# Which engine writes the low parts of U's first 64 tiles: GpSimd without a break during the search's maxima, VectorE during its sums and key choice

## The chip, the core and the metric

One core of a Trainium2 chip runs the whole program: two transformer-like blocks on 256 tokens of width 1024, in fp32. The time is device microseconds of one launch; before the change the median of three runs is 1352.74 us (1351.55 to 1354.43). TensorE multiplies, VectorE and ScalarE do elementwise work, GpSimd can do elementwise work too, and SyncE's queue (SP) starts most transfers from memory.

## The reference, cut to what matters

The stretch in question is the mixture of 16,384 experts at the end of the first block. Each of 8 heads picks 16 experts from two sets of 128 keys; each token then uses 128 rows of `expert_u` and `expert_v`.

```
q = (xn @ w_query).reshape(bsz, seq, PEER_HEADS, 2, PEER_HALF)
scores = einsum("bshpd,hpnd->bshpn", q, sub_keys)
s_top, i_top = lax.top_k(scores, PEER_TOPK)              # 16 of 128, twice a head
cand = s_top[..., 0, :, None] + s_top[..., 1, None, :]
cand_idx = i_top[..., 0, :, None] * PEER_KEYS + i_top[..., 1, None, :]
best, pos = lax.top_k(cand, PEER_TOPK)
idx = take_along_axis(cand_idx, pos); gates = softmax(best)
act = gelu(einsum("td,ted->te", xt, expert_u[it]))
y = einsum("te,ted->td", gt * act, expert_v[it])
```

The kernel does not gather: it multiplies the tokens with all of U (128 tiles of 128 experts), and sets the gates to zero where an expert was not picked.

## The kernel before, in words

**Split weights.** A product in fp32 is made of three faster ones. Each weight tile (128 x 1024, 512 KB) is loaded by SP's queue into a buffer `raw`. ScalarE writes its high part `hi` (`split_next`, L140), and VectorE or GpSimd the low part `lo = raw - hi` (L142). TensorE then does, for each of 8 blocks of the tile, hi with the tokens' high part, hi with their low part, and lo with their high part (L153 to L155): 24 matmuls a tile. `raw`, `hi` and `lo` have three buffers each, so the high part of tile n+3 waits until TensorE is done with tile n, and a load waits until both parts of the tile three before have been read out.

**Who does the low part.** `plan()` lists all tiles in the order of their use and notes for each whether GpSimd ("G") or VectorE ("V") does its low part. In all other weights it is VectorE. In the first 64 tiles of U the pattern is "GGGV".

**What runs beside it.** While TensorE works on U's first 64 tiles, VectorE finds the experts (`topk`, started by `side`). It works in two rounds of 128 tokens. A round is: the maxima (16 times MAX, MAX_INDEX, MATCH_REPLACE, MAX, MAX_INDEX on 128 scores, L1089 to L1094); the candidate sums (`cand`, L1103, and `sif`, L1109); the maxima of the candidates (L1112 to L1117); and the key choice: `ex` (L1123), whose exponential ScalarE takes (L1124), `ab`, `abf`, `fb` (L1128 to L1142), sums and scaling (`sm`, `exk`, L1145 to L1149), and for each of the two key sets a comparison `oh` with all 16 places (L1155), its product with the indices (L1157), and four halvings (L1160, L1161). The results are transposed on TensorE and copied to `iT`, `jT`, `gh`, `gl` (L1170 to L1173). Next `modulation` begins: 96 loads of `wm` (L1321) from GpSimd's queue, each followed by a weighted sum on VectorE (L1324), which frees the one buffer for the next load. `gates` makes R, E, Ch and Cl (L1199 to L1205), two sets ahead of their use.

**What orders it.** The generators advance one step at a tick, two ticks a tile. A scheduler then places each instruction in its engine's queue; the queues run in order. `behind` puts each step of `topk` behind the last low part that VectorE has been given:

```
i = (self.G if self.order[m][1] else self.V).tensor_sub(lo, raw, hi.bitcast(F32))
if not self.order[m][1]:
    self.last_split = i
...
with self.tc.issue_after(self.last_split.ins):
    r = next(gen)
```

Tiles of U are numbered from 0 here. Gelu (L1179) takes the product of two tiles (a pair) from one of two buffers, and TensorE needs that buffer again two pairs later.

Of the kernel before, what the change touches and what calls it, by code (L numbers as in the profile page):

```python
# [40 lines left out]
class Net:  # L41
# [26 lines left out]
    def plan(self):  # L68

        I = self.I  # L70
        w = I["w_in"]
        o = []

        self.first_ring, self.second_ring = [], []
        bufs = {id(self.first_ring): 3, id(self.second_ring): 1}

        def add(tiles, who, deep=False):
            for n, t in enumerate(tiles):
                ring = self.second_ring if deep and n % 4 == 0 else self.first_ring
                o.append((t, who[n % len(who)] == "G", ring, ring[-bufs[id(ring)]] if len(ring) >= bufs[id(ring)] else -1))  # L80
                ring.append(len(o) - 1)
        add([I["w_xk"][b] for b in range(8)], "V")
        add([I["w_ba"]] + [w[b] for b in range(16, 20)], "V")
        add([I["w_xv"][b] for b in range(4)], "V")
        add([w[b] for b in (*range(12, 16), *range(20, 24))], "V")
        add([I["w_xv"][b] for b in range(4, 8)], "V")
        add([w[b] for b in range(24, 28)], "V")
        add([w[b] for i in range(4) for b in (4 + i, 8 + i)], "V")
        add([w[b] for b in range(0, 4)], "V")
        add([I["w_out"][b] for b in range(8)], "V")  # L90
        add([I["w_xq"][b] for b in range(8)], "V", True)
        add([I["w_xo"][b] for b in range(8)], "V", True)
        add([I["w_pq"][b] for b in range(8)], "V", True)
        add([I["U"][b] for b in range(64)], "GGGV")
        add([I["U"][b] for b in range(64, 128)], "V")
        add([I["V"][b] for b in range(64)], "V")
        add([I["V"][b] for b in range(64, 128)], "V")
        for g in range(4):
            add([I["cv_ab"][4 * g + b] for b in range(4)], "V")
        add([I["cv_g"][b] for b in range(8)], "V")  # L100
        add([I["cv_out"][b] for b in range(8)], "V", True)
        add([I["pl_in"][b] for b in range(16)], "V", True)
        add([I["pl_grp"][b] for b in range(2)], "V")
        add([I["pl_out"][b] for b in range(8)], "V", True)
        self.order = o
        self.pos = self.n_dma = self.n_split = 0
        self.raws, self.tiles = {}, {}
# [1705 lines left out]
```

## Time and profile before

| | |
|---|---|
| median of 3 runs | 1352.74 us |
| profiled execution | 1357.57 us, span 1355.0 us |
| TensorE busy | 1295.6 us (96%), 11212 matmuls |
| VectorE busy | 1013.2 us (75%) |
| ScalarE busy | 643.0 us (47%) |
| GpSimd busy | 182.4 us (13%), of it 120.4 in 48 low parts (2513 ns mean) |
| VectorE's low parts | 343, 424.6 us (1241 ns mean) |
| mean granted clock of TensorE | 0.983 of full speed |

The chain of work that ended last lies on TensorE for 84% of the span and on VectorE for 9%. Busy shares are means over the whole program; the change lies between 315 and 525 us, where the first 64 tiles of U are multiplied.

### The profile page before, as it was taken

How to read it: one execution, taken by the hardware profiler on the slowest of the kernel's cores; microseconds unless marked ns; L12 is line 12 of the kernel's file. 1: busy time of each engine (PE TensorE's matmuls, PEld its weight loads, DVE VectorE, ACT ScalarE, POOL GpSimd, SP SyncE). 2: the span in 40 equal slices, each digit the busy share in tenths (PEclk: the TensorE clock that was granted, in tenths of full speed). 3: DMA queues.
4: the chain of work that ended last, by engine and by line, in shares of the span. 5: the costliest groups of instructions: out<-in, count | busy, mean ns of one | idle time of the engine just before them, and what ended most of it. 6: DMA issues, size and time to landing. Idle time of an engine off the chain costs nothing.

```text
span 1355.0 us, 27261 instructions
## 1 busy us (share of the span) xinstructions
PE 1295.6 (96%) x11212; PEld 1264.5 (93%) x11212; DVE 1013.2 (75%) x1881; ACT 643.0 (47%) x841; POOL 182.4 (13%) x179
## 2 busy tenths in 40 slices
PE   7999979999979989999999999998999999998987
PEld 7999969989979989999999999998999996998987
DVE  7897756456897856888887999985666666667885
ACT  6675335555444534443444434434444444455652
POOL 0000000002655663000000000010000000000000
PEclk9999998999999999999999999998999997999999
DMA  7644324444546656666767676666777772433553
GB/s 237 199 149 127 94 79 155 126 140 140 172 132 190 178 163 224 207 210 206 214 202 222 211 213 198 209 215 207 235 235 233 235 225 70 129 130 111 171 163 118
DMA packets 67340, 239.69 MB, mean 177 GB/s; under 512 B 8146, under 2 KB 8402, under 8 KB 67088
## 3 DMA queue, kind: packets, MB, share of 16 engines
q1 hardware_dynamic: 59536, 212.79, 51.7%
q0 software_dynamic: 7680, 25.17, 5.6%
q8 instruction: 87, 1.43, 0.4%
q14 instruction: 37, 0.30, 0.1%
HBM read 236.88 MB, written 1.05 MB: 176 GB/s over the span
## 4 chain that ended last, share of the span: by engine, by line
PE 84%; DVE 9%; ACT 2%; DMA 2%; issue 2%; SPq 0%; DVEq 0%; ACTq 0%
PE mm L155 12%; PE mm L153 12%; PE mm L154 12%; PE y L1261 9%; PE y L1263 9%; PE y L1262 9%; DVE lo L142 3%; PE mm L185 2%; PE mm L186 2%; PE mm L184 2%; PE mmv L210 1%; PE mmv L212 1%; PE mmv L211 1%; PE G L1213 1%; ACT hi L140 1%
## 5 line engine op out<-in xcount | busy, mean ns | idle before, releaser
L140 ACT ACTIVATE hi<-raw 128x1024 fp32r<-128x1024 f32 x391 | 412.5, 1060 | 565.8 <-PE mm L154 221.9
L142 DVE TENSOR_TENSOR lo<-raw,hi 128x1024 fp32r<-128x1024 f32 x343 | 424.6, 1241 | 182.4 <-ACT hi L140 181.5
L155 PE MATMUL mm<-xbh,lo 128*128 128x256 f32 x1128 | 319.0, 283 | 12.3 <-DVE lo L142 12.2
L153 PE MATMUL mm<-xbh,hi 128*128 128x256 f32 x1128 | 321.1, 285 | 0.9 <-ACT act L1179 0.6
L154 PE MATMUL mm<-xbl,hi 128*128 128x256 f32 x1128 | 317.7, 282 | 0.0
L1261 PE MATMUL y<-xbh,hi 128*128 128x256 f32 x1008 | 285.3, 284 | 3.8 <-ACT hi L140 3.8
L1262 PE MATMUL y<-xbl,hi 128*128 128x256 f32 x1008 | 284.5, 283 | 0.0
L1263 PE MATMUL y<-xbh,lo 128*128 128x256 f32 x1008 | 283.8, 282 | 0.8 <-DVE lo L142 0.8
L155 PEld LDWEIGHTS mm<-xbh,lo 128*128 128x128 f32 x1128 | 213.9, 190 | 13.7 <-DVE lo L142 13.5
L153 PEld LDWEIGHTS mm<-xbh,hi 128*128 128x128 f32 x1128 | 214.4, 190 | 1.4 <-ACT act L1179 0.8
L154 PEld LDWEIGHTS mm<-xbl,hi 128*128 128x128 f32 x1128 | 214.4, 190 | 0.0
L1261 PEld LDWEIGHTS y<-xbh,hi 128*128 128x128 f32 x1008 | 191.1, 190 | 4.0 <-ACT hi L140 4.0
L1263 PEld LDWEIGHTS y<-xbh,lo 128*128 128x128 f32 x1008 | 190.6, 189 | 1.7 <-DVE lo L142 1.0
L1262 PEld LDWEIGHTS y<-xbl,hi 128*128 128x128 f32 x1008 | 191.3, 190 | 0.0
L142 POOL TENSOR_TENSOR lo<-raw,hi 128x1024 fp32r<-128x1024 f32 x48 | 120.4, 2513 | 198.4 <-ACT hi L140 198.1
L153 PE MATMUL mm<-xah,hi 128*128 128x256 f32 x448 | 128.5, 288 | 3.4 <-ACT xah L1384 3.4
L154 PE MATMUL mm<-xal,hi 128*128 128x256 f32 x448 | 127.9, 286 | 0.7 <-DVE xal L1385 0.7
L155 PE MATMUL mm<-xah,lo 128*128 128x256 f32 x448 | 127.9, 286 | 0.5 <-DVE lo L142 0.5
L1321 POOL DMA_DIRECT2D wm<-in_w_mod x96 | 51.7, 539 | 531.1 <-DVE wm L1324 515.3
L153 PEld LDWEIGHTS mm<-xah,hi 128*128 128x128 f32 x448 | 85.0, 190 | 4.7 <-ACT xah L1384 3.6
L155 PEld LDWEIGHTS mm<-xah,lo 128*128 128x128 f32 x448 | 85.1, 190 | 1.8 <-issue 1.0
L154 PEld LDWEIGHTS mm<-xal,hi 128*128 128x128 f32 x448 | 84.9, 190 | 1.8 <-DVE xal L1385 0.9
(463 smaller groups left out, 2183.8 us busy)
## 6 DMA issues: line engine op xcount, KB each, us to landing
raw<-in_U SPq DMA_DIRECT2D x128, 512.0 KB, 3.8
raw<-in_V SPq DMA_DIRECT2D x128, 512.0 KB, 4.2
wm<-in_w_mod POOLq DMA_DIRECT2D x96, 256.0 KB, 4.0
raw<-in_w_in SPq DMA_DIRECT2D x28, 512.0 KB, 3.7
raw<-in_cv_ab SPq DMA_DIRECT2D x16, 512.0 KB, 3.6
raw<-in_pl_in SPq DMA_DIRECT2D x16, 512.0 KB, 4.3
raw<-in_w_xk SPq DMA_DIRECT2D x8, 512.0 KB, 4.9
raw<-in_w_xv SPq DMA_DIRECT2D x8, 512.0 KB, 4.2
```

What stands on the lines that cost most here:

```text
L140: self.A.activation(hi, raw, AF.Copy)
L142: i = (self.G if self.order[m][1] else self.V).tensor_sub(lo, raw, hi.bitcast(F32))
L153: self.P.matmul(ps, lhsT=hi[:, w], rhs=xh[:, k, :], start=(k == 0 and first), stop=False, skip_group_check=True)
L154: self.P.matmul(ps, lhsT=hi[:, w], rhs=xl[:, k, :], start=False, stop=False, skip_group_check=True)
L155: self.last_mm = self.P.matmul(ps, lhsT=lo[:, w], rhs=xh[:, k, :], start=False, stop=(k == KB - 1), skip_group_check=True)
L184: self.P.matmul(o, lhsT=hi[:, c], rhs=xh[:, k, :], start=a, stop=False, skip_group_check=True)
L185: self.P.matmul(o, lhsT=hi[:, c], rhs=xl[:, k, :], start=False, stop=False, skip_group_check=True)
L186: self.P.matmul(o, lhsT=lo[:, c], rhs=xh[:, k, :], start=False, stop=z, skip_group_check=True)
L1261: P.matmul(o, lhsT=hi[:, w], rhs=wh[:, s, :], start=(j == 0 and db % 2 == 0), stop=False, skip_group_check=True)
L1262: P.matmul(o, lhsT=hi[:, w], rhs=wl[:, s, :], start=False, stop=False, skip_group_check=True)
L1263: P.matmul(o, lhsT=lo[:, w], rhs=wh[:, s, :], start=False, stop=(j == 127), skip_group_check=True)
L1321: nc.gpsimd.dma_start(w, self.I["w_mod"][n, :, 512 * c:512 * (c + 1)])
```

## The change

The pattern "GGGV" of U's first 64 tiles is replaced by a list of tiles that are VectorE's; all others are GpSimd's.

```diff
-        add([I["U"][b] for b in range(64)], "GGGV")
+
+        mine = (12, 13, *range(18, 26), 39, 40, *range(45, 53))
+        add([I["U"][b] for b in range(64)], ["V" if b in mine else "G" for b in range(64)])
```

VectorE has 20 of the 64 tiles instead of 16: 12 and 13 in the first round's sums, 18 to 25 in its key choice, 39, 40 and 45 to 52 in the second round. GpSimd has 0 to 11, 14 to 17, 26 to 38, 41 to 44 and 53 to 63 without a break. Since `behind` follows VectorE's last low part, the queues change too. In after, line numbers below the diff are two higher (L142 becomes L144).

VectorE's queue in the first round's key choice, of before, from the comparison of the first key set on (the low part at the end is tile 23's; tile 19's stands two rows ahead of the first):

```order
L1155 TENSOR_TENSOR oh<-abf,iota_3604 128x2048
L1146 RECIPROCAL sm<-sm 128x8
L1157 TENSOR_TENSOR oh<-oh,sif 128x2048
L1147 TENSOR_SCALAR sm<-sm 128x8
L1160 TENSOR_TENSOR oh<-oh 128x1024
L1149 TENSOR_TENSOR exk<-ex,sm 128x8x16
L1160 TENSOR_TENSOR oh<-oh 128x512
L1160 TENSOR_TENSOR oh<-oh 128x256
L1161 TENSOR_TENSOR sel<-oh 128x128
L1155 TENSOR_TENSOR oh<-abf,iota_3604 128x2048
L142 TENSOR_TENSOR lo<-raw,hi 128x1024
```

The same place in after, from the third low part of the choice on (the low parts are those of tiles 20 to 23):

```order
L144 TENSOR_TENSOR lo<-raw,hi 128x1024
L1159 TENSOR_TENSOR oh<-oh,sif 128x2048
L1149 TENSOR_SCALAR sm<-sm 128x8
L144 TENSOR_TENSOR lo<-raw,hi 128x1024
L1162 TENSOR_TENSOR oh<-oh 128x1024
L1151 TENSOR_TENSOR exk<-ex,sm 128x8x16
L1162 TENSOR_TENSOR oh<-oh 128x512
L1162 TENSOR_TENSOR oh<-oh 128x256
L144 TENSOR_TENSOR lo<-raw,hi 128x1024
L1163 TENSOR_TENSOR sel<-oh 128x128
L1157 TENSOR_TENSOR oh<-abf,iota_3604 128x2048
L144 TENSOR_TENSOR lo<-raw,hi 128x1024
```

Ahead of tile 23's low part stood ten instructions of the choice in a row; now at most four stand between two low parts.

GpSimd's queue around the second round's end, of before (`lo` are low parts, `wm` the modulation's loads):

```order
L923 TENSOR_TENSOR oT<-oT,zs 128x512 x2
L142 TENSOR_TENSOR lo<-raw,hi 128x1024 x45
L1321 DMA wm<-in_w_mod 128x512
L142 TENSOR_TENSOR lo<-raw,hi 128x1024
L1321 DMA wm<-in_w_mod 128x512
L142 TENSOR_TENSOR lo<-raw,hi 128x1024 x2
L1321 DMA wm<-in_w_mod 128x512 x61
```

And of after:

```order
L925 TENSOR_TENSOR oT<-oT,zs 128x512 x2
L144 TENSOR_TENSOR lo<-raw,hi 128x1024 x39
L1323 DMA wm<-in_w_mod 128x512
L144 TENSOR_TENSOR lo<-raw,hi 128x1024 x2
L1323 DMA wm<-in_w_mod 128x512
L144 TENSOR_TENSOR lo<-raw,hi 128x1024 x2
L1323 DMA wm<-in_w_mod 128x512
L144 TENSOR_TENSOR lo<-raw,hi 128x1024
L1323 DMA wm<-in_w_mod 128x512 x60
```

The first load still stands behind tile 58's low part; behind it there are now two low parts (59 and 60) before the second load, two before the third (61 and 62) and one behind it (63).

VectorE's queue at the same place, of before, from the last copy of the search on:

```order
L1173 TENSOR_TENSOR gl<-ptk,gh 128x128
L1316 TENSOR_SCALAR silu_c<-silu_c 128x512
L1317 SCALAR_TENSOR_TENSOR silu_c<-tanh_c,silu_c 128x512
L142 TENSOR_TENSOR lo<-raw,hi 128x1024
L1324 SCALAR_TENSOR_TENSOR wm,part<-wm,silu_c 128x512 x2
L142 TENSOR_TENSOR lo<-raw,hi 128x1024 x2
L1324 SCALAR_TENSOR_TENSOR wm,part<-wm,silu_c 128x512
L142 TENSOR_TENSOR lo<-raw,hi 128x1024 x2
L1324 SCALAR_TENSOR_TENSOR wm,part<-wm,silu_c 128x512
```

And of after, up to the low parts of tiles 65 and 66:

```order
L1175 TENSOR_TENSOR gl<-ptk,gh 128x128
L1318 TENSOR_SCALAR silu_c<-silu_c 128x512
L1319 SCALAR_TENSOR_TENSOR silu_c<-tanh_c,silu_c 128x512
L1326 SCALAR_TENSOR_TENSOR wm,part<-wm,silu_c 128x512 x2
L1205 TENSOR_TENSOR Ch<-E,gh 128x512
L1201 TENSOR_TENSOR R<-iota,iT 128x1024
L1207 TENSOR_TENSOR Cl<-E,gl 128x512
L1203 TENSOR_TENSOR E<-iota,jT 128x512
L144 TENSOR_TENSOR lo<-raw,hi 128x1024
L1326 SCALAR_TENSOR_TENSOR wm,part<-wm,silu_c 128x512
L144 TENSOR_TENSOR lo<-raw,hi 128x1024 x2
L1326 SCALAR_TENSOR_TENSOR wm,part<-wm,silu_c 128x512
```

The low parts of tiles 59 and 63 are gone from VectorE, the first two weighted sums follow each other, and four instructions of the gates stand ahead of tile 64's low part.

## Rows read from the trace of the kernel before

**Rows 1.** TensorE's waits, 315 to 525 us: waited for, total us, times, longest.
```profile
PE mm L155 <- DVE lo L142: 11.2, 3, 4.9
```

**Rows 2.** Timeline of TensorE, 373 to 494: start, us, instruction, [idle before, releaser].
```profile
373.39 0.28 PE L154 MATMUL mm<-xbl,hi 128*128 128x256 f32 x1
375.22 0.39 PE L155 MATMUL mm<-xbh,lo 128*128 128x256 f32 x1 [1.54 <-DVE lo L142]
...
383.52 0.28 PE L155 MATMUL mm<-xbh,lo 128*128 128x256 f32 x1
384.42 0.39 PE L153 MATMUL mm<-xbh,hi 128*128 128x256 f32 x1 [0.62 <-ACT act L1179]
...
399.24 0.28 PE L154 MATMUL mm<-xbl,hi 128*128 128x256 f32 x1
404.34 0.58 PE L155 MATMUL mm<-xbh,lo 128*128 128x256 f32 x1 [4.82 <-DVE lo L142]
...
408.31 0.28 PE L155 MATMUL mm<-xbh,lo 128*128 128x256 f32 x1
...
411.95 0.28 PE L153 MATMUL mm<-xbh,hi 128*128 128x256 f32 x1
...
485.26 0.28 PE L154 MATMUL mm<-xbl,hi 128*128 128x256 f32 x1
490.39 0.58 PE L155 MATMUL mm<-xbh,lo 128*128 128x256 f32 x1 [4.86 <-DVE lo L142]
...
493.69 0.28 PE L155 MATMUL mm<-xbh,lo 128*128 128x256 f32 x1
```

**Rows 3.** Windows: us, each engine's busy time, granted clock, DMA share, GB/s.
```profile
381.00:407.00 26.00, 20.48 (x158) 19.86 (x157) 25.62 (x25) 11.89 (x14) 15.59 (x6) 0.89 0.41 116
402.00:403.00 1.00, 0.00 (x0) 0.00 (x0) 1.00 (x1) 0.00 (x0) 1.00 (x1) 0.50 0.00 0
409.00:410.00 1.00, 1.00 (x11) 1.00 (x10) 0.00 (x0) 1.00 (x2) 0.00 (x0) 1.00 0.92 377
```

**Rows 4.** Timeline of ScalarE, 342 to 394.
```profile
342.03 1.06 ACT L140 ACTIVATE hi<-raw 128x1024 fp32r<-128x1024 f32 x1 [1.73 <-PE mm L154]
...
381.10 0.40 ACT L1124 ACTIVATE ex<-ex,rcol 128x128 f32<-128x128 f32 x1 [5.33 <-DVE ex L1123]
...
393.63 1.06 ACT L140 ACTIVATE hi<-raw 128x1024 fp32r<-128x1024 f32 x1 [0.67 <-PE mm L155]
```

**Rows 5.** Timeline of VectorE, 372 to 471.
```profile
372.08 3.09 DVE L142 TENSOR_TENSOR lo<-raw,hi 128x1024 fp32r<-128x1024 f32 x1
...
382.75 2.81 DVE L1142 TENSOR_TENSOR abf<-bi,fb 128x128 f16<-128x128 uint32 x1
...
397.54 3.46 DVE L1155 TENSOR_TENSOR oh<-abf,iota 128x2048 f16<-128x2048 f16 x1
400.93 3.36 DVE L142 TENSOR_TENSOR lo<-raw,hi 128x1024 fp32r<-128x1024 f32 x1
...
412.82 1.23 DVE L142 TENSOR_TENSOR lo<-raw,hi 128x1024 fp32r<-128x1024 f32 x1 [5.56 <-ACT hi L140]
...
470.75 0.74 DVE L1142 TENSOR_TENSOR abf<-bi,fb 128x128 f16<-128x128 uint32 x1
```

**Rows 6.** Timeline of GpSimd, 343 to 421.
```profile
343.17 2.39 POOL L142 TENSOR_TENSOR lo<-raw,hi 128x1024 fp32r<-128x1024 f32 x1 [0.38 <-ACT hi L140]
...
400.46 2.74 POOL L142 TENSOR_TENSOR lo<-raw,hi 128x1024 fp32r<-128x1024 f32 x1 [0.54 <-ACT hi L140]
...
415.96 5.34 POOL L142 TENSOR_TENSOR lo<-raw,hi 128x1024 fp32r<-128x1024 f32 x2 [3.56 <-ACT hi L140]
```

**Rows 7.** Timeline of GpSimd, 517 to 523.
```profile
517.68 0.55 POOL L1321 DMA_DIRECT2D wm<-in_w_mod  x1 [2.03 <-DVE wm L1324]
518.26 4.77 POOL L142 TENSOR_TENSOR lo<-raw,hi 128x1024 fp32r<-128x1024 f32 x2
```

**Rows 8.** Loads of U issued, 330 to 372: KB each, median us to landing.
```profile
raw<-in_U SPq DMA_DIRECT2D x13, 512.0 KB, 3.6
```

## The prediction

> **What bounds the kernel now.** I read the page first: TensorE is busy 96% of the span and its waits are the only idle time that counts. Then I asked for TensorE's waits in the stretch that the diff touches, the first 64 tiles of U (315 to 525 us). There the low parts were late on VectorE three times, 11.2 us in all [rows 1]. The timeline of TensorE [rows 2] turns this into lost time. Undisturbed, 31 matmuls start between 408.31 and 411.95, one each 0.117 us, so a tile of 24 takes 2.82 us. Four places fall off that pace:
> - 373.39 to 375.22: 1.83 us for one pitch, 1.7 lost.
> - 383.52 to 384.42: 0.90 us, 0.8 lost, behind a Gelu on ScalarE (L1179).
> - 399.24 to 404.34: 5.10 us, 5.0 lost. Then 18 matmuls start in 3.97 us (404.34 to 408.31) where 2.12 would do: 1.85 lost. The granted clock is 0.50 there and 1.00 afterwards [rows 3]: TensorE had stood idle, fell from 2.4 to 1.2 GHz, and worked some 4 us before it was back.
> - 485.26 to 490.39: 5.13 us, 5.0 lost, and 15 matmuls in 3.30 us (490.39 to 493.69) instead of 1.76: 1.5 lost.
> Sum: 1.7 + 0.8 + 5.0 + 1.85 + 5.0 + 1.5 = 15.9 us, 1.2% of the span.
>
> The reader is to see next why a low part is late. The high part of tile 23 starts on ScalarE at 393.63 and TensorE wants the low part some 5.7 us later, at 399.24 [rows 2, 4]; VectorE starts it at 400.93 [rows 5]. It stands in VectorE's queue behind the key choice, and those instructions are long: L1142 takes 2.81 us at 382.75 and 0.74 at 470.75; a low part takes 1.23 at 412.82 but 3.36 at 400.93, when GpSimd is inside a low part of its own (400.46, 2.74 long) [rows 5, 6]. From 382.75 to 400.93 there are six such instructions of 2.3 us or more, the first and the last of which are shown. The two engines hold each other up, and VectorE loses about 2.1 us each time. GpSimd suffers less: 2.39 us at 343.17 beside maxima, 2.74 at 400.46 [rows 6].
>
> **The change part by part.**
> *Tiles 18 to 25 and 45 to 52 on VectorE during the sums and the key choice.* GpSimd is then idle, so the lengthening goes. VectorE is busy 25.62 of the 26 us from 381 to 407 [rows 3]. Taking off six times 2.1 (12.6) leaves 13.0, of which two low parts are 2.5, so the choice itself is about 10.5 us. Eight low parts of 1.23 make 9.8: 20.3 us of work in eight tiles (22.6 us). It fits with 2 us over. In the order of after the 10.5 us stand in pieces between the low parts, 1.3 us on the mean; the longest piece, the seven instructions from L1123 to L1142, I estimate at under 3, since L1142 alone is 0.74. A VectorE low part is ready 1.06 + 0.1 + 1.23 = 2.4 us after its high part starts and is wanted 5.7 us after: 3.3 us of cover. So both 5 us waits go, and with them both stretches at 1.2 GHz: 13.4 us. If the cover fails, one tile's wait of 5 us comes back.
> *Tiles 12, 13 and 39, 40 on VectorE during the candidate sums.* The first wait (tile 15) came of it: VectorE was behind with sums lengthened by GpSimd, started tile 15 at 372.08 although its high part was long there, and then took 3.09 us itself [rows 5]. Now tile 15 is GpSimd's and the sums have VectorE alone: 1.7 us go. ScalarE stood 5.33 us at the exponential of the chosen scores (381.10, L1124), waiting for a late VectorE, with Gelu and two high parts queued behind [rows 4]; that made the 0.8 us wait. In after the exponential's operand follows tile 18's low part directly, and ScalarE's table load covers that. So 0.8 go.
> *36 tiles plus eight as GpSimd's alone during the maxima.* The cost of a lone run is 2.4 us a tile on GpSimd against 2.82 on TensorE, so it keeps pace. Latency: the high part starts at 342.03, the low part ends at 345.56 [rows 4, 6], 3.5 us later, wanted after 5.7: 2.2 us of cover. The maxima themselves do not lengthen it: 2.39 us is measured beside a full VectorE queue. Taken as nothing. Bounds: 0, and if each stood at the 2.74 of a contended one, still under 2.82: also 0.
> *Nine two-operand instructions of the gates* (R, E, Ch, Cl, L1199 to L1205) stand among the second round's maxima in both orders. In before the two of L1199 met a pair of low parts (415.96), which took 5.34 instead of 4.8 us [rows 6], 0.27 for each instruction. Nine times 0.27 is 2.4 us of lag against 2.2 of cover, and if one low part bears both, 0.54 each, 4.9: between 0 and 2.7 us. I take 0.2, near the row itself, since gaps of 0.4 us between low parts let GpSimd catch up.
> The Trainium skill, "SBUF — State Buffer", section "SBUF: two separate sides", says that VectorE instructions with two SBUF inputs, or in a two-port mode, and GpSimd's share one port pair, which the first to start holds for its whole instruction. The six long instructions agree with that. By that rule the nine instructions would hold GpSimd for their full lengths, and the sum would be worse by up to about 2 us than with the 0.27 of the row; no run here shows which it is in an unbroken GpSimd run.
> *Tiles 53 to 63 on GpSimd, with three of the modulation's loads in its queue.* This is the one place that gets tighter. The load of wm waits for VectorE's sum over the previous one, and the low parts behind it on GpSimd's queue wait too. In before the second load waited 2.03 us (517.68), and the next two low parts ran back to back, 4.77 us [rows 7]; TensorE just did not wait. Now tiles 59 and 63 also go through GpSimd (in before VectorE did them), 2.4 us each, with the second load between 60 and 61 and the third between 62 and 63. Following the queue with before's durations, tile 61's low part ends 0.3 us and tile 63's 0.85 us too late, and tile 64's, behind four gate instructions on VectorE, about level. Bounds: 0, and 4 us (two waits of 2.03 passed on in full). I take 1.0.
> *What else is queued.* A raw buffer is free only after the low part has read it, and GpSimd's low part ends 1.2 us later than VectorE's. The round trip of three buffers is landing 3.6 us [rows 8] + high part 1.06 + low part 2.4 + about 0.4 of hand-overs = 7.5 us for three tiles, which TensorE takes 8.46 for. Hidden, 1.0 us of cover. SP's order of loads is the same. Behind tile 64 only neighbours change places in VectorE's order, where TensorE has no low-part waits now: nothing.
> Sum: 13.4 + 1.7 + 0.8 - 0.2 - 1.0 = 14.7 us gained.
> The profiled execution took 1357.57 us with a span of 1355.0, 4.8 us above the runs' median of 1352.74; the waits lie in the program, so I take the 14.7 us off both: 1342.9 for its like, and 1352.74 - 14.7 = **1338.0 us** for the median.
>
> **The rivals.**
> *GpSimd runs late in places.* For it: 2.03 us wait before the load, tight already, and the nine gate instructions. Against: 2.2 us of cover elsewhere. If the two loads' waits come in full (4), the nine cost 2, and one stretch falls to 1.2 GHz again (1.85 + about 2), 5 to 10 us of the 15.9 are eaten: 1342 to 1347.
> *VectorE's instructions in the choice are not shortened.* If their length had another cause than GpSimd, the choice needs 23.1 us, with eight low parts 32.9 in 22.6 us: 10.3 late less 3.3 of cover, 7.0 a round, with the slow clock 8.7; twice that is 17.4 for 15.9 taken away: 1354, no change. Against: the same line, L1142, at 2.81 and 0.74 in the same program.
> *The buffers' round trip becomes the bound (slower).* Place: all-GpSimd runs, 44 tiles, some 14 round trips. If landing rises over 4.6 us, each 1 us more costs 14 us; above 4.6 + 15.9/14 = 5.7 us the kernel is slower than before. At 6.2 it gives 1338 + 22 = 1360. For it: nothing breaks up the runs any more. Against: landing 3.6 us beside the same loads now.
>
> **How the numbers follow.** Forecast (1334 to 1342): 0.68. Late GpSimd (1342 to 1348): 0.19. No shortening: 0.06. Round trip or something like it: 0.05. Better than 1334: 0.02. The likeliest gives 1338. Its bounds are 1336.8 (nothing lost in the loads or the gates) and some 1342 (4.0 in the loads and a little of the 2.7 in the gates); the other cases reach on, so the range is 1333 to 1347, which leaves out the last two rivals. A measurement of this kernel can tell about 0.2% (2.7 us) from no change. Faster: 0.68 + 0.19 + 0.02 = 0.89; within 0.2%: 0.06; slower: 0.05.
>
> **What would show it.** Right: no wait of TensorE on a low part above 1 us before tile 53; granted clock 1.00 through both key choices; low parts of tiles 18 to 25 at 1.23 us and L1142 at 0.74; GpSimd's low parts at 2.4 beside maxima; ScalarE idle under 1 us before the exponential. Wrong: low parts or choice instructions above 2 us with GpSimd idle; GpSimd back to back without gaps in the maxima; high parts waiting for loads of U; TensorE waiting for GpSimd between tiles 59 and 64 by more than 2 us.

## The result and the profile after

The changed kernel takes 1340.1 us (median of 4 runs, 1339.7 to 1340.9) where the kernel before took 1353.6 (4 runs beside it, 1351.6 to 1354.6): a ratio of 0.9897, 95% interval [0.9876, 0.9917], 13.5 us by the medians. The forecast was 1338.0, 1333 to 1347. The profiled execution took 1340.44 us with a span of 1338.2.

Between 300 and 530 us TensorE has no wait left in the list of waits; [rows 1] has no answer there. These are rows of the list over the whole program; the last, on low parts (five waits, the longest 0.5 us), lies elsewhere:

```profile
PE mm L155 <- ACT hi L142: 7.7, 2, 7.4
...
PE y L1263 <- ACT hi L142: 5.0, 1, 5.0
...
PE mm L157 <- DVE lo L144: 2.3, 5, 0.5
```

The windows that answer to [rows 3] (us; busy time and count of TensorE, its weight loads, VectorE, ScalarE, GpSimd; granted clock; DMA share, GB/s): TensorE is busy throughout, and the clock stays at 1.00, 2.4 GHz, where it was 0.50.

```profile
381.00:407.00 26.00, 26.00 (x224) 26.00 (x224) 25.08 (x86) 13.71 (x16) 7.00 (x3) 1.00 0.65 187
402.00:403.00 1.00, 1.00 (x10) 1.00 (x10) 1.00 (x9) 0.00 (x0) 1.00 (x1) 1.00 0.65 66
```

VectorE's timeline in the first key choice (start, duration in us, line, instruction; lines have moved by two, so L142 of [rows 5] is L144 and L1142 is L1144). The cast of the choice is 0.75 us here and 2.81 in [rows 5], the comparison (now L1157) 1.22 instead of 3.46, the low parts 1.17 to 1.44 instead of 3.36. From 381 to 407 us VectorE is as busy as before (25.08 us for 25.62), but six low parts start there instead of two, and the choice is done at 398 us instead of 407:

```profile
376.66 1.22 DVE L144 TENSOR_TENSOR lo<-raw,hi 128x1024 fp32r<-128x1024 f32 x1 [4.16 <-ACT hi L142]
...
379.76 0.75 DVE L1144 TENSOR_TENSOR abf<-bi,fb 128x128 f16<-128x128 uint32 x1
380.12 1.44 DVE L144 TENSOR_TENSOR lo<-raw,hi 128x1024 fp32r<-128x1024 f32 x1
...
381.66 1.22 DVE L1157 TENSOR_TENSOR oh<-abf,iota 128x2048 f16<-128x2048 f16 x1
...
393.51 1.23 DVE L144 TENSOR_TENSOR lo<-raw,hi 128x1024 fp32r<-128x1024 f32 x1 [0.46 <-ACT hi L142]
```

ScalarE's timeline at the exponential, which stood 5.33 us in [rows 4] and follows its table load at once here:

```profile
377.13 1.28 ACT L1126 ACT_TABLE_LOAD   x1
378.42 0.40 ACT L1126 ACTIVATE ex<-ex,rcol 128x128 f32<-128x128 f32 x1
```

GpSimd's timeline, first beside the gate instructions ([rows 6]), then at the modulation's loads ([rows 7]). Its low parts are up to 0.25 us longer beside a gate instruction, with gaps of 0.16 to 0.77 ahead of them. The three loads that have low parts behind them wait 0.9 to 1.7 us for VectorE (the fourth, shown last, 2.8), and the first two pairs of low parts behind them run without a gap, but TensorE waits for none:

```profile
410.84 2.65 POOL L144 TENSOR_TENSOR lo<-raw,hi 128x1024 fp32r<-128x1024 f32 x1 [0.77 <-ACT hi L142]
413.65 2.41 POOL L144 TENSOR_TENSOR lo<-raw,hi 128x1024 fp32r<-128x1024 f32 x1 [0.16 <-ACT hi L142]
416.47 2.47 POOL L144 TENSOR_TENSOR lo<-raw,hi 128x1024 fp32r<-128x1024 f32 x1 [0.41 <-ACT hi L142]
...
500.48 0.56 POOL L1323 DMA_DIRECT2D wm<-in_w_mod  x1 [0.88 <-DVE wm L1326]
501.06 4.76 POOL L144 TENSOR_TENSOR lo<-raw,hi 128x1024 fp32r<-128x1024 f32 x2
...
512.47 0.55 POOL L1323 DMA_DIRECT2D wm<-in_w_mod  x1 [2.80 <-DVE wm L1326]
```

### The profile page after: what moved, and what is told of

Its sections match the earlier page's. It is cut to its first block, busy times and chain, and to the rows that moved or that the text cites. A ratio compares the mean times of both kernels' runs of the same rounds, so it can differ in the third digit from the quotient of the medians.

```text
span 1338.2 us, 27259 instructions
## 1 busy us (share of the span) xinstructions
PE 1291.0 (96%) x11212; PEld 1262.5 (94%) x11212; DVE 988.9 (74%) x1885; ACT 643.1 (48%) x841; POOL 168.0 (13%) x175
## 4 chain that ended last, share of the span: by engine, by line
PE 90%; DVE 4%; ACT 2%; DMA 2%; issue 1%; SPq 0%; DVEq 0%; ACTq 0%
PE mm L155 14%; PE mm L157 14%; PE mm L156 14%; PE y L1263 9%; PE y L1265 9%; PE y L1264 9%; DVE lo L144 2%; PE mmv L212 2%; PE mm L187 2%; PE mmv L214 2%; PE mmv L213 2%; PE mm L188 2%; PE mm L186 2%; PE G L1215 1%; PE G L1216 1%; DMA raw<-in_V 1%
## 5 line engine op out<-in xcount | busy, mean ns | idle before, releaser
L142 ACT ACTIVATE hi<-raw 128x1024 fp32r<-128x1024 f32 x391 | 412.7, 1060 | 554.8 <-PE mm L156 229.0
L144 DVE TENSOR_TENSOR lo<-raw,hi 128x1024 fp32r<-128x1024 f32 x347 | 423.8, 1224 | 184.0 <-ACT hi L142 182.8
L144 POOL TENSOR_TENSOR lo<-raw,hi 128x1024 fp32r<-128x1024 f32 x44 | 106.1, 2413 | 199.4 <-DVE mt L1094 123.5
L1326 DVE SCALAR_TENSOR_TENSOR wm<-wm,silu_c 128x512 f32<-128x512 f32 x96 | 68.9, 718 | 25.0 <-DMA wm<-in_w_mod 24.6
```

The source lines that it names most:

```text
L142: self.A.activation(hi, raw, AF.Copy)
L1326: V.scalar_tensor_tensor(w, w, 1.0, s, op0=OP.mult, op1=OP.mult, accum_out=part[:, n, c:c + 1])
```

## The experiments

The theory: VectorE and GpSimd hold each other up, so VectorE's choice grows and the low parts behind it in its queue come late. The rivals: the gain came of the sums, of four tiles more on VectorE, or of another order of VectorE's work. The first three kernels and the two with one engine alone change only the pattern of the kernel before (tile numbers b of U, "V" for VectorE).

**The key choice alone.**
```diff
-        add([I["U"][b] for b in range(64)], "GGGV")
+        add([I["U"][b] for b in range(64)], ["V" if b % 4 == 3 or 18 <= b < 26 or 45 <= b < 53 else "G" for b in range(64)])
```


> Only the key choice is changed: tiles 18 to 25 and 45 to 52 go to VectorE, all others stay in the old pattern of three and one. If the two long waits came of GpSimd's low parts lengthening VectorE's choice, 13.4 of the 15.9 us lost go in the profile, and of the 13.5 us by which the runs' medians fell some 11.5: about 1341 to 1343 us; no TensorE wait of 5 us is left, and the one of about 1.7 us at tile 15 stays. If it was the sums that delayed VectorE into the choice, most of the gain is missing: about 1350.

Measured: 1342.6 us against 1355.8 for before: 13.2 us by the medians, some 11 by the ratio of 0.9917 [0.9893, 0.994]. The list of TensorE's waits from 300 to 540 us has one row, tile 15's (so the wait behind the Gelu is gone as well), and VectorE's timeline shows its low part held up to 3.09 us by GpSimd, as in [rows 5]:

```profile
PE mm L155 <- DVE lo L142: 1.5, 1, 1.5
```
```profile
371.83 3.09 DVE L142 TENSOR_TENSOR lo<-raw,hi 128x1024 fp32r<-128x1024 f32 x1
```

**The sums alone.**
```diff
+        add([I["U"][b] for b in range(64)], ["V" if b % 4 == 3 or b in (12, 13, 39, 40) else "G" for b in range(64)])
```


> Only the candidate sums are changed: tiles 12, 13, 39 and 40 go to VectorE as well, the rest stays in the old pattern. If the choice is what costs, the two waits of some 5 us at tiles 23 and 55 stay and only 1.7 to 2.5 us go: 1351 to 1352. If the delay is made in the sums and only shows later, both long waits go: about 1340 to 1343.

Measured: 1349.0, ratio 0.9955 [0.9937, 0.9973]: 6.8 us by the medians, some 6 by the ratio, between the two expectations. In the timeline of VectorE instructions of the choice are held up as before (2.84, 2.37 and 3.41 us), but it starts 2.8 us earlier (L1142 at 379.97, not 382.75), and TensorE's two waits shrink to 4.3 us in all:

```profile
379.97 2.84 DVE L1142 TENSOR_TENSOR abf<-bi,fb 128x128 f16<-128x128 uint32 x1
...
388.45 2.37 DVE L1147 TENSOR_SCALAR sm<-sm 128x8 f32<-128x8 f32 x1
...
396.03 3.41 DVE L142 TENSOR_TENSOR lo<-raw,hi 128x1024 fp32r<-128x1024 f32 x1
```
```profile
PE mm L155 <- DVE lo L142: 4.3, 2, 2.5
```

So the sums hand their delay on to the choice. By the medians the two parts alone gain 13.2 and 6.8 us, 20.0 together, and both at once 13.5; by the ratios it is some 17 against 14, which the intervals do not tell apart. The traces do, with one execution of each kernel. From its first Gelu to its last, U takes 377.8 us with the choice alone and 381.8 with the sums alone (the rows below: count, shortest, median and longest ns, first and last start); with both it takes 375.3, and before 392.3 and 388.4 in two executions (the rows are shown further down). Against the shorter of these the parts gain 10.6 and 6.6, 17.2 together, and both at once 13.1; against the longer, 25.0 and 17.0. They take from one backlog and don't add up.

```profile
L1179 ACT ACTIVATE act<-mm x64: 569/581/600, 338.5 to 716.3; 128x512 f32<-128x512 f32 x64
```
```profile
L1179 ACT ACTIVATE act<-mm x64: 575/581/599, 340.0 to 721.8; 128x512 f32<-128x512 f32 x64
```

**Twenty tiles on VectorE, but spread evenly.**
```diff
+        add([I["U"][b] for b in range(64)], ["V" if b % 16 in (3, 6, 9, 12, 15) else "G" for b in range(64)])
```


> As many low parts on VectorE as in the changed kernel (20 of 64), but spread evenly (tiles 3, 6, 9, 12 and 15 of every 16), so that GpSimd has five or six of the eight tiles of either key choice. If the place counts, VectorE's instructions in the choice stay at 2.3 us and more where GpSimd meets them and TensorE waits 3 to 5 us in each: 1348 to 1356. If it is only that VectorE, the faster engine at a low part, takes four tiles more: about 1340.

Measured: 1356.6, ratio 1.0017 [0.9998, 1.0036]. TensorE's waits between 300 and 540 us:

```profile
PE mm L155 <- DVE lo L142: 9.2, 3, 4.4
```
The number of tiles gains nothing; where they stand does.

**GpSimd busy beside the choice, all else as in the changed kernel.**
```diff
+        b = m - self.u0
+        if 18 <= b < 26 or 45 <= b < 53:
+            if b == 18:
+                self.dum = self.top.tile([128, 1024], F32, name="dum")
+                self.G.memset(self.dum, 0.0)
+            self.G.tensor_sub(self.dum, self.dum, hi.bitcast(F32))
```


> The changed kernel, its low parts where they are, and beside each of the 16 tiles of the key choices one more instruction on GpSimd that nobody waits for (it takes the tile's high part from a scratch tile, 128x1024 and two operands like a low part; its result is not used). VectorE's order is untouched. If GpSimd's work alone lengthens VectorE's, the choice instructions and VectorE's low parts that meet it go to 2.3 us and more; VectorE has 20.3 us of work in 22.6 us there and would get up to 8 times 2.1 on top, 11 us too much a round after the cover: TensorE waits some 5 to 11 us in each round, with the slow clock 1352 to 1366. If the changed order of VectorE's work made the gain, nothing happens: 1340.

Measured: 1369.6, ratio 1.0115 [1.0091, 1.0139], 29.5 us above the changed kernel and slower than before. TensorE's waits, VectorE's timeline (lines here are 7 further: L1132 is the difference ahead of the exponential, 0.29 us in the timeline of the kernel with the choice alone, L1164 the comparison), and the group of extra instructions on GpSimd (a low part of that size takes 2.4 us; busy us, mean ns, idle before):

```profile
PE mm L164 <- DVE lo L145: 19.4, 8, 4.6
```
```profile
376.70 2.49 DVE L1132 TENSOR_TENSOR ex<-bv 128x128 f32<-128x128 f32 x1
...
380.87 2.85 DVE L1151 TENSOR_TENSOR abf<-bi,fb 128x128 f16<-128x128 uint32 x1
383.33 3.34 DVE L145 TENSOR_TENSOR lo<-raw,hi 128x1024 fp32r<-128x1024 f32 x1
...
386.79 3.19 DVE L1164 TENSOR_TENSOR oh<-abf,iota 128x2048 f16<-128x2048 f16 x1
```
```profile
L153 POOL TENSOR_TENSOR dum<-dum,hi 128x1024 f32<-128x1024 f32 x16 | 45.5, 2843 | 23.7 <-ACT hi L143 23.4
```
VectorE does the same instructions in the same order, and only GpSimd's work is new; it reads `hi`, but no high part on ScalarE waits for it. That shows the cause: GpSimd's work beside the choice, by itself, costs more than the change gains, and the changed order of VectorE's queue alone gains nothing. The old order without GpSimd beside it was not tried.

**The same extra work in four pieces.**
```diff
+            for c in range(0, 1024, 256):
+                self.G.tensor_sub(self.dum[:, c:c + 256], self.dum[:, c:c + 256], hi[:, c:c + 256].bitcast(F32))
```


> The last one with each of the 16 extra GpSimd instructions cut into four of 128x256 (0.6 to 0.85 us each by the smaller two-operand instructions of the trace; the same columns in all, results not used). If a VectorE instruction that meets one of GpSimd's stands until that one has ended, as the 2.37 us of a 128x8 instruction in the even spread read, the excess of a meeting falls from up to 2.4 us to 0.85 at most, and VectorE's backlog to a third or so: 1340 to 1352. If the two share what they read through, the excess goes with the columns, and the time stays at 1365 to 1372, or rises with the four times as many starts.

Measured: 1367.7, ratio 1.0115 [1.0096, 1.0134]. The time speaks for the second reading, the rows for the first. The 128x8 instruction, 0.16 us alone (L1149 of the changed kernel) and 2.37 beside whole instructions, is 0.70 here, and no low part of the first choice is over 1.76:

```profile
388.71 0.70 DVE L1157 TENSOR_SCALAR sm<-sm 128x8 f32<-128x8 f32 x1
...
398.06 1.76 DVE L145 TENSOR_TENSOR lo<-raw,hi 128x1024 fp32r<-128x1024 f32 x1
```
As these rows read, a meeting costs VectorE about the rest of the GpSimd instruction in progress. But GpSimd now pays: a piece takes 1163 ns, four of them 4.65 us a tile where TensorE takes 2.82, so it works without a pause and its real low parts, queued behind, come late as well. TensorE waits less for VectorE and newly for GpSimd. A second effect comes in: the pieces read `hi`, whose buffer is free only behind them, and six high parts on ScalarE wait 19.8 us for that. So the time of this run does not decide between the two readings (first the pieces' group, then TensorE's waits from 300 to 540 us and ScalarE's from 360 to 500):

```profile
L154 POOL TENSOR_TENSOR dum<-dum,hi 128x256 f32<-128x256 f32 x64 | 72.1, 1163 | 0.4 <-ACT hi L143 0.4
```
```profile
PE mm L165 <- DVE lo L145: 10.3, 12, 2.1
PE mm L165 <- POOL lo L145: 7.0, 3, 3.3
```
```profile
ACT hi L143 <- POOL dum L154: 19.8, 6, 5.3
```

**All low parts on GpSimd** (the pattern "G").

> All 64 low parts on GpSimd. VectorE's choice is then lengthened at every tile, but no low part is queued behind it. If the cost comes from low parts that stand in VectorE's queue behind a lengthened choice, TensorE hardly waits: GpSimd needs 2.4 to 2.8 us a tile (3.1 the longest seen) for TensorE's 2.82, with 2.2 us of cover: 1338 to 1346. If GpSimd falls behind when it is held up at every tile, or the late choice itself is waited for, 1350 and more.

Measured: 1370.3, ratio 1.0133 [1.0114, 1.0152]; the first expectation failed. GpSimd does keep pace: TensorE waits 0.6 us for it over 64 tiles. What it waits for are Gelus on ScalarE, and in ScalarE's timeline they stand behind the second round's exponential, which waits 22.41 us for VectorE's sums and maxima, high parts queued behind it (last row: the same exponential in the kernel before):

```profile
PE mm L153 <- ACT act L1179: 23.1, 2, 19.5
PE mm L155 <- POOL lo L142: 0.6, 1, 0.6
```
```profile
392.15 1.28 ACT L1124 ACT_TABLE_LOAD   x1
415.85 0.40 ACT L1124 ACTIVATE ex<-ex,rcol 128x128 f32<-128x128 f32 x1 [22.41 <-DVE ex L1123]
```
```profile
465.12 0.40 ACT L1124 ACTIVATE ex<-ex,rcol 128x128 f32<-128x128 f32 x1
```
VectorE is not late here: it is 49 us ahead of the kernel before. With none of U's low parts in its queue, `behind` no longer ties the search to these tiles, and the scheduler puts this exponential 24 high parts earlier on ScalarE (the first round's six earlier). ScalarE then stands at it, and TensorE behind ScalarE. So VectorE's result can cost TensorE time by a second way, with no low part in its queue; but most of this run's 30 us above the changed kernel may be the price of that order, and the run does not show what contention alone costs.

**All low parts on VectorE** (the pattern "V").

> All 64 low parts on VectorE, GpSimd has none. Nothing lengthens VectorE's instructions any more, but it takes 44 low parts of 1.23 us more, 54 us, beside the search and the choice. If being alone were all that counts, 1338 to 1342. If the load counts as well, VectorE has some 184 us of work in 181 and falls behind during the maxima: TensorE waits 5 to 15 us in pieces, 1345 to 1356.

Measured: 1341.1, ratio 0.9902 [0.9885, 0.9919], not to be told from the changed kernel. TensorE has no wait from 300 to 540 us. The group of VectorE's low parts in 315 to 540 us, and the window of the second round's maxima:

```profile
L142 DVE TENSOR_TENSOR lo<-raw,hi 128x1024 fp32r<-128x1024 f32 x76 | 93.0, 1224 | 22.8 <-ACT hi L140 22.5
```
```profile
410.00:460.00 50.00, 50.00 (x423) 50.00 (x423) 49.81 (x207) 23.46 (x27) 0.00 (x0) 1.00 0.60 182
```
The expected 184 us of work in 181 was wrong: over four windows from 315 to 500 us VectorE is busy 163.6 of 185. It is full (49.81 of 50) only in this one, and in time all the same. What GpSimd does in the changed kernel is worth nothing that these runs can tell.

**Every second tile of the choice back on GpSimd.**
```diff
-        mine = (12, 13, *range(18, 26), 39, 40, *range(45, 53))
+        mine = (12, 13, 18, 20, 22, 24, 39, 40, 45, 47, 49, 51)
```


> The changed kernel with every second tile of the two key choices (19, 21, 23, 25 and 46, 48, 50, 52) given back to GpSimd. VectorE then has 10.5 us of choice and 4.9 us of low parts in 22.6 us, 7 us of slack, and meets four of GpSimd's instructions, up to 2.1 us each. If backlog is what counts, TensorE waits little, 0 to 3 us in all: 1340 to 1344. If each meeting costs TensorE something by itself, or the evenly spread kernel's waits of 9.2 us come back: 1346 to 1356.

Measured: 1347.9, ratio 0.9948 [0.9933, 0.9963], in the second expectation's range, but neither names the place. TensorE waits for no low part. It waits once, for the choice's result: its own transpose of the selected keys stands in its queue, and VectorE comes to the result late. Three of its last instructions for it were held up by some 2 us each (3.43 for the comparison, 2.89 and 2.46 for halvings), and some 7 us of the second round's maxima now stand between the last four, from 399.4 to 409.4 us; which of the two made the 4.07 us was not tried. In TensorE's timeline, and then VectorE's:

```profile
410.42 0.48 PE L1170 MATMUL ptk<-ident,sel 128*128 128x128 f32 x1 [4.07 <-DVE sel L1163]
```
```profile
390.81 3.43 DVE L1157 TENSOR_TENSOR oh<-abf,iota 128x2048 f16<-128x2048 f16 x1
```
Some 13 matmuls after it run at 1.2 GHz (granted clock 0.50). The backlog is smaller and shows at a third place.

**The kernel before once more.** No edit.

> The kernel before once more, for a second profile. If the size of its two long waits differs from execution to execution (which instruction of VectorE meets which of GpSimd's is a matter of tenths of a us), the waits of TensorE on VectorE's low parts between 315 and 525 us sum to another number than 11.2, by several us, and the time goes with it. If they are the same to some tenths, the scatter of its runs, 1349 to 1361, has another cause.

Measured: 1349.6 in one run; its waits on low parts sum to 9.0 us instead of 11.2. The list of waits, the window that answers to the clock of 0.50 in [rows 3], and TensorE's row at the first long wait:

```profile
PE mm L155 <- DVE lo L142: 9.0, 3, 4.9
```
```profile
402.00:403.00 1.00, 1.00 (x9) 1.00 (x10) 1.00 (x1) 0.00 (x0) 1.00 (x1) 1.00 0.54 61
```
```profile
401.88 0.39 PE L155 MATMUL mm<-xbh,lo 128*128 128x256 f32 x1 [2.50 <-DVE lo L142]
```
The first long wait is 2.50 us here, where it was 4.82 in [rows 2], and the clock did not fall after it. 23 runs of before beside the first experiments reach from 1348.9 to 1360.7; the changed kernel's four lie within 1.2 us.

**A wait outside the change.** In both kernels TensorE waits some 4 to 5 us near 914 us for a late load of V. Two tries on the changed kernel, each moving loads from SP's queue to GpSimd's:
```diff
-        nc.sync.dma_start(inv, I["inv"])
+        nc.gpsimd.dma_start(inv, I["inv"])
```


> The changed kernel, and the load of the inverse table (L1363) is issued by GpSimd in place of SP, where it waits at 903.65 us for a buffer and holds back the loads of V behind it. TensorE's wait of 5.0 us at 913.82 should go, with some 1 to 2 us at the slow clock behind it: 1333 to 1336. If those loads are late for another cause, no change: 1340.

Measured: 1340.7, ratio 0.9909 [0.9894, 0.9925]: no change. The load of V was late as before (ScalarE's timeline), so the inverse table was the wrong suspect:

```profile
913.99 1.06 ACT L142 ACTIVATE hi<-raw 128x1024 fp32r<-128x1024 f32 x1 [9.11 <-DMA raw<-in_V]
```
```diff
-        nc.sync.dma_start(self.ftap, I["ftap"])
+        nc.gpsimd.dma_start(self.ftap, I["ftap"])
...
-        nc.sync.dma_start(self.dw, I["cv_dw"])
+        nc.gpsimd.dma_start(self.dw, I["cv_dw"])
```


> The changed kernel; the small loads of the tap tables (L1344 and L1346) are issued by GpSimd in place of SP. With the inverse's load moved, TensorE's wait of 5 us near 914 us stayed, the load of V behind these two landed 14.9 us after its issue, and the core's transfers ran at 23 to 42 GB/s for some 6 us. If V's loads stand behind the two tables in their queue, the wait goes: 1333 to 1337. If the tables hold up the transfers wherever they are issued, no change: 1340.

Measured: 1332.1, ratio 0.9833 [0.9814, 0.9852], better than both kernels and just under the first expectation's range. TensorE has no wait left from 860 to 960 us. Times from issue to landing (min, median, max) of the raw tiles, 885 to 918 us in the changed kernel, and 880 to 918 in this one:

```profile
DMA to landing us min/median/max: 3.6/4.5/15.3
```
```profile
DMA to landing us min/median/max: 3.4/4.3/5.3
```

## Why the prediction was right

Right in sign, mechanism and range; the size was 2.1 us off.

- **Choice, 13.4 us.** Alone it gained 13.2 by the medians, 8 to 14.5 by the ratio's interval. Low parts at 1.17 to 1.44 us, the cast at 0.75 and the clock at 1.00 came as written. That GpSimd's work is the cause is shown by putting it back (29.5 us slower).
- **Sums, 1.7 and 0.8 us.** With the choice already changed the 1.7 is about what was said: the wait of 1.5 us is left at tile 15, and the choice alone is 2.5 us above both together (the intervals of the two ratios overlap; U's time differs by 2.5 too). The 0.8 behind the Gelu belongs to the choice: it went with the choice alone. Alone the sums are worth some 6: the sum treated its terms as independent, and they share VectorE's backlog.
- **Nine gate instructions, 0.2 us.** At most 0.25 us on a GpSimd low part and no wait. The prediction priced only GpSimd's side, and it is VectorE that pays: six of the nine take 1.97 to 2.62 us in the changed kernel where 0.41 to 0.68 is their length alone, some 10 us in all (the row below is the longest, 0.42 alone). It costs nothing because no low part stands in VectorE's queue there. The Trainium skill, "SBUF — State Buffer", section "SBUF: two separate sides", has the first to start hold the shared ports for its whole instruction. On VectorE's side the runs agree (0.16 us becomes 2.37 beside an instruction of 2.4 us, 0.70 beside a piece), and at all six gate instructions GpSimd had started first. So the up to 2 us that the prediction took from it did not come.

```profile
411.15 2.62 DVE L1203 TENSOR_TENSOR E<-iota,jT 128x512 f16<-128x512 f16 x1
```
- **The modulation's loads, 1.0 us.** They wait as foreseen, and TensorE doesn't: 0.
- **The base.** This is the step that was mis-sized. 15.9 us were lost in one execution of before, 4.8 us over the median, and the 14.7 were taken off the median too. By the first and last of U's 64 Gelus (the groups of before, before again and after; first and last start), U takes 392.3, 388.4 and 375.3 us: the loss itself differs by 3.9 us between two executions. The 17.0 us of the first pair is more than 14.7 by the two deductions, 1.2, which were nothing, and by 1.1 that the list of waits doesn't hold. The second execution of before, 3 us under the first median, loses 13.1 against the changed kernel. So the 13.5 us between the medians is read as a typical execution that loses less than the profiled one; two executions are all that there is for it.

```profile
L1179 ACT ACTIVATE act<-mm x64: 569/581/599, 338.8 to 731.1; 128x512 f32<-128x512 f32 x64
```
```profile
L1179 ACT ACTIVATE act<-mm x64: 573/581/601, 338.6 to 727.0; 128x512 f32<-128x512 f32 x64
```
```profile
L1181 ACT ACTIVATE act<-mm x64: 574/581/601, 338.5 to 713.8; 128x512 f32<-128x512 f32 x64
```

Of the rivals, VectorE's instructions did shorten; GpSimd was not late, and even all 64 tiles on it made TensorE wait 0.6 us for low parts; and the raw buffers' round trip bounded nothing: from 315 to 525 us six high parts waited for loads of U, 12.2 us in all, where five waited 16.7 before, and TensorE for none of them. What no part of the prediction saw is that VectorE alone does as well: its argument that GpSimd keeps pace was true and not needed. Which of VectorE's instructions are held up by GpSimd and which are not was read in passing only, and not tried one by one.

## What to carry to other kernels

An engine that helps can cost more than it does: before giving GpSimd a share, look for the same line of VectorE at two durations, and time the version without the helper. Terms that draw on one backlog don't add; cost the late consumer, and look for every queue in which the late engine's result is awaited, here VectorE's own, ScalarE's exponential and TensorE's transposes. A change of who does the work can move other instructions in the queues too, so read the order before a time is put down to contention. A stall that comes of two engines meeting differs from execution to execution, so its size in one profile is a sample, to be set against the scatter of the runs.

## What the hardware showed that was not expected

With two tables of 31 partitions, 62 and 124 KB, ahead of it in SP's queue, a tile of 512 KB took 15.3 us from issue to landing, where the median is 4.5. In the profile's rates over time the core moved 23 to 28 GB/s for some 6 us meanwhile. The Trainium skill, "DMA: Bandwidth & Descriptors", section "Why a DMA increments its semaphore by 16 and not by 1", says that a transfer uses the largest number of engines up to 16 that divides the slowest dimension (of more than one element) on both sides: for 31 that is one. The low rate agrees. Issued by GpSimd the same two tables let the tiles land in 5.3 us at most; they land in 4.6 and 6.1 us themselves, and no stretch of 6 us at such a rate is left. So it is not shown whether the other queue helped or another way of spreading the tables. The rates around the late tile, 40 slices of 885 to 920 us in the changed kernel:

```profile
GB/s 164 412 248 0 122 351 126 56 197 375 318 126 332 262 328 234 360 342 384 384 339 173 102 342 156 300 375 112 28 28 23 28 23 28 23 98 295 220 5 0
```
